# A hybrid convolution and RWKV-7 block on one core: the turns of even and odd chunks in the inverse's two merging bursts

## The chip, the cores and the metric

The kernel runs on one core of one Trainium2 chip. Its time is the device time of one execution in microseconds. The number given for a kernel is the median of several executions; the profile comes from one more execution. The engines are TensorE (PE, with its weight loads shown apart as PEld), VectorE (DVE), ScalarE (ACT), GpSimd (POOL) and SyncE (SP), which issues the transfers.

## The reference, cut to what matters

The block has 2048 tokens and 1024 channels. A normalised, modulated input goes through one wide projection. From it come a convolution branch (gate, causal depthwise convolution of width 31, layer norm) and an RWKV-7 branch with 16 heads of 64, whose state is updated token by token. Both are gated, projected, added, projected again, and normalised.

```python
def step(state, inp):
    r_t, w_t, k_t, v_t, kk_t, b_t = inp
    sk = jnp.einsum('bhvk,bhk->bhv', state, kk_t)
    state = (state * w_t[:, :, None, :] - sk[..., None] * b_t[:, :, None, :]
             + v_t[..., None] * k_t[:, :, None, :])
    return state, jnp.einsum('bhvk,bhk->bhv', state, r_t)
...
p = jnp.einsum('bsd,de->bse', h, w_in[l])
c_val, c_gate, c_og, ts, r_og, g_conv, g_rwkv = jnp.split(p, SPLITS, axis=-1)
y_conv = _conv_branch(c_val, c_gate, c_og, ...)
y_rwkv = _rwkv7_branch(ts, r_og, ...)
m = jax.nn.sigmoid(g_conv) * y_conv + jax.nn.sigmoid(g_rwkv) * y_rwkv
x = x + gate[:, None, :] * jnp.einsum('bsd,de->bse', m, w_out[l])
```

## The kernel before, in words

The tokens are worked on in four blocks of 512 (`TB`), the blocks in chunks of 64 tokens (`CH`, eight to a block), and the heads in four groups of four (`group`, two pairs `q` of two heads `hh`). So `group` runs sixteen times. Beside it, each block's wide projection and convolution are computed (`project`, `conv`, `gates`); the projection's products, `mm3k` at L205, are most of PE's instructions, and each weight tile of 128 columns is split into a high and a low part (`load_w`, L188 and L190). After the four blocks a second phase does the output projections.

Inside a chunk the recurrence is replaced by a triangular system: `As` holds, for each chunk, a 64 by 64 triangular matrix that has to be inverted. `group` does so for its 32 matrices (two pairs, two heads, eight chunks) at once:

- The two diagonal 32 by 32 blocks of each matrix go out to memory (`dA`, L610) and come back as `La`, where GpSimd inverts all of them together in 31 steps (L624, L626). The inverses go out again (`dT`) and come back into `As` (L637).
- The off-diagonal block of the inverse is the product of three 32 by 32 blocks. VectorE transposes one of the diagonal inverses into `T11` (L652, eight transposes, each for one pair, one head and the chunks of one parity). A first burst of 32 products on PE (L656) writes `pq`, a PSUM tile that the trace names `late`. VectorE copies it to `Qs` (L660, one copy per parity). A second burst of 32 products (L665) writes `pq` again, and VectorE copies the result into `As` (L670).
- Then the chunks are gone through one after another: L683, L685, L688, L690, L694 and L698 carry the state `S` on.

Even and odd chunks (`e`, 0 and 1) lie on different partitions. For an even chunk `quarters(e)` gives 64 to 95 and 96 to 127, for an odd one 0 to 31 and 32 to 63. The first burst reads from the first of the two ranges and writes to the second, the second burst the other way round.

The order of instructions on each engine is not the order of the text. A scheduler runs over the whole program, simulates the engines, and writes out the order that comes of it; on the chip each engine then executes its own list in order. So L205's products of the projection stand between the steps of the inverse and of the recurrence.

Of the kernel before, what the change touches and what calls it, by code (L numbers as in the profile page):

```python
# [82 lines left out]
def hybrid_block(ctx: ExitStack, tc: tile.TileContext, x, vecs, convk, w2a2, final_g, ada, w_in, w_co, w_ro, w_o, crow, out,  # L83
# [491 lines left out]
    def group(b, g, h, lora, fill):  # L575
# [14 lines left out]
        for c4 in range(NCH // 4):  # L590
            pv = pa.tile([P, 2, 2, P], F32, name="aux", tag="aux")
            for c in range(4 * c4, 4 * c4 + 4):
                e = c % 2
# [48 lines left out]
        def quarters(e):  # L642
            p0 = 64 - 64 * e
            return slice(p0, p0 + 32), slice(p0 + 32, p0 + 64)

        every = [(q, hh, c) for q in range(2) for hh in range(2) for c in range(NCH // 2)]
        pq = pl.tile([P, 2, 2, NCH // 2, 32], F32, name="late", tag="late")
        for e in range(2):
            lo_, hi_ = quarters(e)
            for q in range(2):  # L650
                for hh in range(2):
                    nc.vector.transpose(T11[lo_, q, hh], As[q][lo_, hh, e::2, lo_])  # L652
        for e in range(2):
            lo_, hi_ = quarters(e)
            for n, (q, hh, c) in enumerate(every):
                nc.tensor.matmul(pq[hi_, q, hh, c, :], As[q][lo_, hh, 2 * c + e, hi_], T11[lo_, q, hh, c, :],  # L656
                                 start=(n == 0), stop=(n == 15), skip_group_check=True)
        for e in range(2):
            lo_, hi_ = quarters(e)
            nc.vector.tensor_copy(Qs[hi_], pq[hi_])  # L660

        for e in range(2):
            lo_, hi_ = quarters(e)
            for n, (q, hh, c) in enumerate(every):
                nc.tensor.matmul(pq[lo_, q, hh, c, :], Qs[hi_, q, hh, c, :], As[q][hi_, hh, 2 * c + e, hi_],  # L665
                                 start=(n == 0), stop=(n == 15), skip_group_check=True)
        for e in range(2):
            lo_, hi_ = quarters(e)
# [5 lines left out]
        for c in range(NCH):  # L674
            cc, e = c // 2, c % 2
# [25 lines left out]
        for c4 in range(NCH // 4):  # L701
            po = pl.tile([P, 2, 2, P], F32, name="late", tag="late")
            with tc.issue_after(last.ins if hasattr(last, "ins") else last):
                for c in range(4 * c4, 4 * c4 + 4):
                    e = c % 2
# [166 lines left out]
    for b in range(NB):  # L872
        h = hprep(b) if b else hprep0(x0, ada_steps())
        lora = lora_split(h)
        for g in groups:
# [29 lines left out]

            wcount[0] = WSH
            group(b, g, h, lora, fill)
            if b == 0 and g == GG:
                for _ in ada_cols(srow, l3, "As", ASB, [((16 + k, 17 + k), (hgate_col[:, k:k + 1], hgate_col[:, k + 1:k + 2]))
# [138 lines left out]
    for b in range(NB):  # L1048
# [7 lines left out]
        for tt in range(NTT):  # L1056
            xh = []
            for half in range(2):
                n = 2 * tt + half
# [97 lines left out]
```

## Time and profile before

| what | us |
|---|---|
| median of three runs | 3070.52 |
| lowest and highest of them | 3058.14, 3070.98 |
| the profiled execution's own time | 3056.37 |
| its span, from first to last instruction | 3054.7 |
| PE busy | 2911.1 (95% of the span) |
| DVE busy | 2045.2 (67%) |
| POOL busy | 1257.3 (41%) |
| ACT busy | 1010.8 (33%) |
| PE busy with L656, 1024 records | 35.9 |
| PE busy with L665, 1024 records | 35.0 |

In the views of the profile a row of instructions gives the line in the kernel, the engine, the operation, what is written and read, the shape, and the count; "128*64" ahead of a shape is the part of the array in use, partitions by columns. An arrow names what ended the idle time ahead of an instruction. A product of float32 operands such as L656's stands there as two records, each with its own weight load.

### The profile page before, as it was taken

Reading aid. Unit: us, or ns where it says so; the run is one execution under the profiler, and the core shown is the slowest. Engines: PE = TensorE matmul, PEld = TensorE weight load, DVE = VectorE, ACT = ScalarE, POOL = GpSimd, SP = SyncE. Lnnn points to the kernel's source line nnn. Section 1 sums busy time; section 2 is a strip of 40 time slices with the busy share of each in tenths; the row PEclk is TensorE's granted clock in tenths of the full one; section 3 lists DMA queues with packets and bytes.
Section 4 is the critical chain, followed back from the end, with each engine's and each line's share of the span. In section 5 each row is a group of like instructions: output and inputs, shape, how many; then the busy total and the mean of one; then the engine's idle time right before and its main releaser. Section 6 shows DMA issues by size and latency. Waiting matters only on the chain.

```text
span 3054.7 us, 64810 instructions
## 1 busy us (share of the span) xinstructions
PE 2911.1 (95%) x25672; PEld 2754.0 (90%) x25672; DVE 2045.2 (67%) x3879; ACT 1010.8 (33%) x1887; POOL 1257.3 (41%) x1788
## 2 busy tenths in 40 slices
PE   6789998999999999999999999999999999899998
PEld 5789898999999998999999998999999978687988
DVE  6676877686766675767677667667689534767333
ACT  4424344433333242324242424232332112333101
POOL 3445455533443435243434355426276004555000
PEclk9999999999999999999999999999999999999999
DMA  8666757774747477648585888646457687989674
GB/s 300 220 233 199 250 198 260 242 236 152 243 142 257 140 248 239 194 139 273 161 276 168 274 276 271 199 157 204 154 184 243 199 277 281 325 294 339 235 277 171
DMA packets 366367, 697.14 MB, mean 228 GB/s; under 512 B 135984, under 2 KB 154736, under 8 KB 366064
## 3 DMA queue, kind: packets, MB, share of 16 engines
q1 hardware_dynamic: 366064, 693.00, 67.9%
q8 instruction: 202, 3.31, 0.5%
q14 instruction: 101, 0.83, 0.1%
HBM read 504.04 MB, written 187.70 MB: 226 GB/s over the span
## 4 chain that ended last, share of the span: by engine, by line
PE 57%; DMA 15%; DVE 12%; POOL 7%; ACT 3%; issue 3%; SPq 2%; DVEq 0%; ACTq 0%; POOLq 0%
PE ps_main L205 40%; DMA w_st<-w_in_t 3%; PE aux L537 3%; DVE acc L774 2%; POOL TT L626 2%; POOL itmp L624 2%; DMA w_gr<-grow_d 2%; DMA w_st<-w_co_t 2%; PE xo L688 2%; PE pout L1078 2%; PE pout L1079 2%; PE pout L1077 2%; DMA w_st<-w_ro_t 1%; PE xo L683 1%; PE xo L694 1%
## 5 line engine op out<-in xcount | busy, mean ns | idle before, releaser
L205 PE MATMUL ps_main<-h_hi,w_hi 128*128 128x256 f32 x4608 | 953.4, 285 | 24.3 <-ACT w_hi L188 16.1
L205 PE MATMUL ps_main<-h_hi,w_lo 128*128 128x256 f32 x4608 | 955.6, 285 | 9.6 <-POOL w_lo L190 6.5
L205 PE MATMUL ps_main<-h_lo,w_hi 128*128 128x256 f32 x4608 | 953.4, 284 | 0.0
L205 PEld LDWEIGHTS ps_main<-h_hi,w_hi 128*128 128x128 f32 x4608 | 718.8, 190 | 33.7 <-ACT w_hi L188 17.3
L205 PEld LDWEIGHTS ps_main<-h_hi,w_lo 128*128 128x128 f32 x4608 | 718.2, 190 | 18.3 <-POOL w_lo L190 7.7
L205 PEld LDWEIGHTS ps_main<-h_lo,w_hi 128*128 128x128 f32 x4608 | 717.7, 190 | 4.8 <-issue 0.2
L774 DVE SCALAR_TENSOR_TENSOR acc<-u,ck,acc 128x512 f32<-128x512 f32 x928 | 698.0, 752 | 19.4
L624 POOL TENSOR_TENSOR itmp<-La,TT 128x126 f32<-128x126 f32 (+22 forms) x496 | 181.9, 367 | 126.7 <-DMA La<-dA 91.1
L626 POOL TENSOR_TENSOR TT<-TT,itmp 128x126 f32<-128x126 f32 (+22 forms) x496 | 190.1, 383 | 36.6
L190 POOL TENSOR_TENSOR w_lo<-w_st,w_hi 128x1024 fp32r<-128x1024 f32 x47 | 113.1, 2407 | 116.5 <-ACT w_hi L188 94.6
L680 ACT ACTIVATE Se<-S,pe 128x128 f32<-128x128 f32 x256 | 89.0, 395 | 198.0 <-DVE S L698 196.9
L537 PE MATMUL aux<-KR,BKz 128*128 128x128 f32 x1024 | 137.9, 283 | 12.4 <-POOL KR L523 6.2
L698 DVE TENSOR_TENSOR S<-xo,Se 64x128 f32<-64x128 f32 x256 | 73.5, 287 | 107.6 <-PE xo L694 96.9
L537 PEld LDWEIGHTS aux<-KR,BKz 128*128 128x128 f32 x1024 | 126.9, 197 | 14.9 <-POOL KR L523 6.8
L188 ACT CAST w_hi<-w_st 128x1024 fp32r<-128x1024 f32 x71 | 74.3, 1047 | 195.9 <-DMA w_st<-w_in_t 159.3
L690 DVE TENSOR_TENSOR uv<-xo,rn 64x256 f32<-64x256 f32 x128 | 53.8, 421 | 103.0 <-PE xo L688 101.6
L539 DVE TENSOR_TENSOR As<-aux,maskA 128x512 f32<-128x512 f32 x128 | 87.3, 687 | 38.4 <-PE aux L537 37.3
L685 DVE TENSOR_TENSOR XO<-xo,XO 128x256 f32<-128x256 f32 x128 | 53.7, 419 | 86.1 <-PE xo L683 70.1
L560 POOL TENSOR_TENSOR vv<-rk,vv 128x512 f32<-128x512 f32 x32 | 43.9, 1372 | 154.3 <-ACT rk L559 148.0
L754 ACT ACTIVATE th<-ps_main 128x512 f32<-128x512 f32 x64 | 38.1, 596 | 206.8 <-PE ps_main L205 150.1
L531 ACT COPY BKz<-BK 64x512 f32<-64x512 f32 x128 | 78.9, 616 | 62.7 <-PE aux L537 39.7
L786 ACT ACTIVATE th<-ps_main 128x512 f32<-128x512 f32 x64 | 38.1, 595 | 182.8 <-PE ps_main L205 172.7
(301 smaller groups left out, 5530.9 us busy)
## 6 DMA issues: line engine op xcount, KB each, us to landing
w_hi<-kh_in SPq DMA_DIRECT2D x219, 512.0 KB, 4.2
w_lo<-kl_in SPq DMA_DIRECT2D x219, 512.0 KB, 5.4
w_st<-w_in_t SPq DMA_DIRECT2D x73, 512.0 KB, 4.7
kh_in<-w_hi SPq DMA_DIRECT2D x71, 512.0 KB, 2.9
kl_in<-w_lo SPq DMA_DIRECT2D x71, 512.0 KB, 4.8
w_hi<-kh_ro SPq DMA_DIRECT2D x32, 512.0 KB, 5.1
w_lo<-kl_ro SPq DMA_DIRECT2D x32, 512.0 KB, 6.1
w_hi<-kh_co SPq DMA_DIRECT2D x32, 512.0 KB, 3.9
```

The source lines that it names most:

```text
L188: nc.scalar.copy(hi, st)
L190: lo_eng.tensor_tensor(out=lo, in0=st, in1=hi.bitcast(F32), op=ALU.subtract)
L205: nc.tensor.matmul(ps[:, qs], ww[:, k, :], aa[k][:, qs], start=(k == 0 and t == 0 and q == 0), stop=(k == KT - 1 and t == 2 and q == ms - ...
L531: nc.scalar.copy(BKz[hs, hh], BK[hs, c4 * 2:c4 * 2 + 2])
L537: nc.tensor.matmul(pA[:, c // 2, es], BKz[:, hh, c // 2, es], KR[:, cc, es], start=(c == 0), stop=(c == 3), skip_group_check=True)
L539: nc.vector.tensor_tensor(out=Asb[:, hh, c4 * 4:c4 * 4 + 4, :].rearrange("p (a e) n -> p a (e n)", e=2), in0=pA, in1=flat(maskA).unsqueeze ...
L624: nc.gpsimd.tensor_tensor(out=tmp[:, :ni, :nt], in0=La[:, j:j + 1, j + 1:].broadcast_to([P, ni, nt]), in1=TT[:, :ni, j:j + 1].broadcast_to ...
L626: nc.gpsimd.tensor_tensor(out=TT[:, :ni, j + 1:], in0=TT[:, :ni, j + 1:], in1=tmp[:, :ni, :nt], op=ALU.add)
L680: nc.scalar.mul(Se[:, q, :], Sg[:, q, :], R[q]["pe"][:, c:c + 1])
L688: nc.tensor.matmul(xo[pr_, q, hs], As[q][pr_, hh, c, kcol(e)], XO[pr_, c, q, hs], start=(q == 0 and hh == 0), stop=(q == 1 and hh == 1), s ...
L698: nc.vector.tensor_tensor(out=Sg[hs, :, hs], in0=xo[hs, 2:4, hs], in1=Se[hs, :, hs], op=ALU.add)
L774: nc.vector.scalar_tensor_tensor(out=acc if i + 1 < HALO else yj, in0=u[:, i:i + TB], scalar=ck[:, j, i:i + 1], in1=acc, op0=ALU.mult, op1 ...
```

## The change

In each of the two bursts the loop over parities goes inside the loop over pair, head and chunk. The products are the same, with the same operands, the same places in `pq`, and the same first and last product for each parity. The transposes and copies around them are as they were.

```diff
-        for e in range(2):
-            lo_, hi_ = quarters(e)
-            for n, (q, hh, c) in enumerate(every):
+        for n, (q, hh, c) in enumerate(every):
+            for e in range(2):
+                lo_, hi_ = quarters(e)
                 nc.tensor.matmul(pq[hi_, q, hh, c, :], As[q][lo_, hh, 2 * c + e, hi_], T11[lo_, q, hh, c, :],
                                  start=(n == 0), stop=(n == 15), skip_group_check=True)
         for e in range(2):
             lo_, hi_ = quarters(e)
             nc.vector.tensor_copy(Qs[hi_], pq[hi_])
 
-        for e in range(2):
-            lo_, hi_ = quarters(e)
-            for n, (q, hh, c) in enumerate(every):
+        for n, (q, hh, c) in enumerate(every):
+            for e in range(2):
+                lo_, hi_ = quarters(e)
                 nc.tensor.matmul(pq[lo_, q, hh, c, :], Qs[hi_, q, hh, c, :], As[q][hi_, hh, 2 * c + e, hi_],
                                  start=(n == 0), stop=(n == 15), skip_group_check=True)
```

What the scheduler makes of it on PE, at the second burst of the third group of the first token block. A row is a product or a run of like ones; in brackets stand the engines or transfer queues that it waits for, here the transfers that brought that pair's and head's part of `As`. Before:

```order
L205 MATMUL ps_main<-h_hi,w_hi 128x256 x2
L665 MATMUL late<-As,Qs 32x32 [waits DMAHW2_49,DVE_49]
L665 MATMUL late<-As,Qs 32x32 x3
L665 MATMUL late<-As,Qs 32x32 [waits DMAHW3_49]
L665 MATMUL late<-As,Qs 32x32 x3
L665 MATMUL late<-As,Qs 32x32 [waits DMAHW3_49]
L665 MATMUL late<-As,Qs 32x32 x3
L665 MATMUL late<-As,Qs 32x32 [waits DMAHW4_49]
L665 MATMUL late<-As,Qs 32x32 x3
L665 MATMUL late<-As,Qs 32x32 [waits DMAHW7_49]
L665 MATMUL late<-As,Qs 32x32 x3
```

With the change:

```order
L205 MATMUL ps_main<-h_lo,w_hi 128x256 x2
L665 MATMUL late<-As,Qs 32x32 [waits DMAHW7_49,DVE_49]
L665 MATMUL late<-As,Qs 32x32 [waits DMAHW4_49]
L665 MATMUL late<-As,Qs 32x32 x6
L665 MATMUL late<-As,Qs 32x32 [waits DMAHW0_49]
L665 MATMUL late<-As,Qs 32x32 [waits DMAHW5_49]
L665 MATMUL late<-As,Qs 32x32 x6
L665 MATMUL late<-As,Qs 32x32 [waits DMAHW0_49]
L665 MATMUL late<-As,Qs 32x32 [waits DMAHW5_49]
L665 MATMUL late<-As,Qs 32x32 x6
```

Before, the first sixteen products are the even chunks', four for each pair and head, with one wait each. Now an even and an odd product stand one behind the other at each pair and head, so two waits follow each other, and then six products without any.

The first burst of the very first group stands in pieces among L205's products, on PE. Before:

```order
L205 MATMUL ps_main<-h_lo,w_hi 128x256 x2
L656 MATMUL late<-T_1570,As 32x32 [waits DVE_49]
L656 MATMUL late<-T_1570,As 32x32 x3
L656 MATMUL late<-T_1570,As 32x32 [waits DVE_49]
L656 MATMUL late<-T_1570,As 32x32 x3
L205 MATMUL ps_main<-h_hi,w_lo 128x256 [waits Pool_49]
```

With the change:

```order
L205 MATMUL ps_main<-h_lo,w_hi 128x256 x2
L656 MATMUL late<-T_1570,As 32x32 [waits DVE_49] x2
L656 MATMUL late<-T_1570,As 32x32 x7
L656 MATMUL late<-T_1570,As 32x32 [waits DVE_49]
L656 MATMUL late<-T_1570,As 32x32 x6
L205 MATMUL ps_main<-h_hi,w_lo 128x256 [waits Pool_49]
```

At the same place there stood eight even products, which wait for two transposes; now eight even and eight odd ones stand there, sixteen in all, and they wait for four. The first burst is in pieces in this group and in the second and third groups of the last token block, before and after; in the other thirteen groups, and in all second bursts, the 32 products stand together. Behind the first burst the scheduler's lists differ in many places on all engines, by rows that stand a little earlier or later; no row is lost or gained.

## The prediction

> **What bounds the kernel now.** I read the page's first part, then the table by stretches, then the timeline and the chain of waits around one pair of bursts.
>
> ```profile
> span 3054.7 us, 64810 instructions
> PE 2911.1 (95%) x25672; PEld 2754.0 (90%) x25672; DVE 2045.2 (67%) x3879; ACT 1010.8 (33%) x1887; POOL 1257.3 (41%) x1788
> 200.00:650.00 450.00, 424.77 (x4041) 410.83 (x4041) 335.39 (x581) 177.51 (x298) 235.28 (x307) 0.96 0.69 230
> 650.00:2450.00 1800.00, 1763.80 (x17207) 1711.71 (x17206) 1271.05 (x2401) 607.54 (x1143) 768.01 (x1240) 0.99 0.65 210
> ```
>
> In the last two rows the first number after the length is PE's busy time. PE is idle for 25.2 of 450 us and then for 36.2 of 1800 us. All sixteen groups lie in these 2250 us, and PE's own queue sets the pace there: an instruction taken off PE is time, unless a wait that is there anyway takes it back.
>
> The two bursts of a group, here the third of the first token block, look so on PE's timeline (start, length with the last instruction's own end, count), on the vector engine's, and in the chain (start, time that the piece adds):
>
> ```profile
> 529.58 0.40 PE L205 MATMUL ps_main<-h_hi,w_lo 128*128 128x256 f32 x2
> 529.81 0.39 PE L205 MATMUL ps_main<-h_hi,w_hi 128*128 128x256 f32 x2
> 530.14 2.11 PE L656 MATMUL late<-T,As 32*32 32x32 f32 x64
> 532.17 0.63 PE L505 MATMUL aux<-bones,sq 128*64 128x2 f32 x16
> 532.74 0.51 PE L205 MATMUL ps_main<-h_lo,w_hi 128*128 128x256 f32 x2
> 537.76 2.11 PE L665 MATMUL late<-As,Qs 32*32 32x32 f32 x64
> ...
> 532.28 1.40 DVE L660 COPY Qs<-late 32x512 f32<-32x512 f32 x2 [3.06 <-PE late L656]
> ...
> 530.21 2.04 PE late L656 x64
> 537.83 2.04 PE late L665 x64
> ```
>
> A product of 32 by 32 stands in the trace as two records, so 32 products are 64. Both bursts lie whole on the chain. The even and the odd half's copies start at 532.28, after the last odd product (530.14 + 2.11 = 532.25): the even half's being ready at half time is not used today.
>
> **What the burst would take with turns.** An even product uses partitions 64 to 95 and writes 96 to 127, an odd one 0 to 31 and 32 to 63 (the second burst the other way round): two separate pieces of the array. Three narrow looks at the same burst show what separate pieces do; each row holds what runs within a 10 ns window, at the middle of the even products, at the change from even to odd, and at the middle of the odd ones:
>
> ```profile
> L656 PE MATMUL late<-T,As x1024: 191/191/212, 195.7 to 2418.1; 32*32 32x32 f32 x171
> L665 PE MATMUL late<-As,Qs x1024: 191/191/257, 205.2 to 2424.0; 32*32 32x32 f32 x171
> 530.41 0.38 PE L656 MATMUL late<-T,As 32*32 32x32 f32 x7
> 530.98 0.38 PE L656 MATMUL late<-T,As 32*32 32x32 f32 x10
> 531.42 0.38 PE L656 MATMUL late<-T,As 32*32 32x32 f32 x7
> ```
>
> One record takes 0.19 us, so in the first row seven start within 0.38 - 0.19 us: six gaps of 31.7 ns. At the change ten start in the same time: the last even and the first odd records run together. A second place in this kernel alternates all the way, the sums of L505, whose chunks go in turn to the two halves of the output; L688 has weights of the same 64 columns and stays on one piece:
>
> ```profile
> 2002.23 0.68 PE L688 MATMUL xo<-XO,As 64*64 64x64 f32 x8
> L688 PE MATMUL xo<-XO,As x1024: 218/218/366, 207.9 to 2516.4; 64*64 64x64 f32 x171
> L505 PE MATMUL aux<-bones,sq x512: 197/198/268, 73.4 to 2286.0; 128*64 128x2 f32 x171
> ```
>
> L688: (0.68 - 0.22) / 7 = 66 ns a record. L505: (0.63 - 0.20) / 15 = 29 ns. Alternating there halves the time, over a whole burst and not only at an edge.
>
> **The sum, part by part.** Nothing is removed or added: the 1024 products, the transposes, the copies and every transfer stay.
>
> First, the bursts. With both pieces at their own rate, each does 32 records: 31 x 31.7 ns + 0.19 us = 1.17 us, with a slower first step 1.2. That is 0.91 us less than 2.11, and there are 32 bursts: -29.1 us. The low end of the gain is PE handing out records no faster than in L505: 63 x 28.7 ns + 0.19 = 2.0 us, 0.11 less, -3.5 us in all. I take the upper end, since the row at the change has 9 gaps in 0.19 us, 21 ns on average, although some of these gaps lie outside the overlap.
>
> The Trainium skill ("TensorE: Matmul & The Clock Gate", section "Wait — 56ns, not 53.3ns?") says that start to start never drops under about 25 ns, however small the product. By it a burst would be 63 x 25 ns + 0.19 = 1.8 us (an estimate from that page) and the change worth -11 us; the 21 ns above speak against it, over ten records only.
>
> Second, the waits. An interleaved first burst needs the odd transposes (L652) as early as the even ones. Where the burst stands late this costs nothing: the third group's last transpose (the last row below) ends 34 us before its burst. In three groups the order starts the burst while transposes are still coming: the first of all, and two in the last token block. Rows of the first (vector engine, then PE), of the last block's third, and for comparison of the third group of the first block:
>
> ```profile
> 195.31 0.49 DVE L652 STREAM_TRANSPOSE T<-As 32x128 f32<-32x128 f32 x2 [2.84 <-DMA As<-dT]
> 196.05 0.63 DVE L652 STREAM_TRANSPOSE T<-As 32x128 f32<-32x128 f32 x2 [0.25 <-DMA As<-dT]
> 195.67 0.69 PE L656 MATMUL late<-T,As 32*32 32x32 f32 x16
> ...
> 2270.02 1.35 DVE L652 STREAM_TRANSPOSE T<-As 32x128 f32<-32x128 f32 x5
> 2275.85 0.29 DVE L652 STREAM_TRANSPOSE T<-As 32x128 f32<-32x128 f32 x1
> 2270.52 0.69 PE L656 MATMUL late<-T,As 32*32 32x32 f32 x16
> ...
> 495.99 0.29 DVE L652 STREAM_TRANSPOSE T<-As 32x128 f32<-32x128 f32 x1
> ```
>
> In the first group the eight products that start at 195.67 need the two transposes of 195.31; with turns that place holds sixteen, which need four, the last done at 196.68. PE stands for up to 0.9 us, with the L205 products of that weight tile queued behind it. For the three groups I take 3 us. Low end 0 (the rest of the fill covers it). High end: PE standing from the burst's start to the last transpose, 2276.14 - 2270.52 = 5.6 us, in each of three, 17 us. I stay near the low end because the rows behind the first products are L205's in every one of them.
>
> Third, the copies. Qs's and As's copies start after the last product already, so nothing is lost by the even half's finishing late; they and all that follows (L665, then L688 of the recurrence) start 0.9 us earlier per burst. If the copies of the even half had been early, 0.7 us of cover (half of 1.40) would be gone in each burst; between the bursts PE has L205 work, 5 us in the third group.
>
> Fourth, what is given back. Saved PE time is lost where PE meets a wait that its own progress doesn't feed. Low end 0. High end: the idle time of 61 us grows by a quarter, 15 us. With 3 groups in the stretch that is 5.6% idle and 13 in the one that is 2.0% idle, I take 3 us, the idle share of the gain (0.056 x 5.5 + 0.02 x 23.7 = 0.8) with room for the rest.
>
> Not in the sum, but in the range: the granted clock.
>
> ```profile
> 530.10:533.80 3.70, 3.70 (x90) 3.61 (x90) 1.48 (x3) 1.76 (x2) 1.84 (x1) 1.00 1.01 314
> 533.80:537.20 3.40, 3.40 (x17) 3.21 (x16) 2.29 (x6) 2.24 (x4) 3.23 (x4) 0.50 0.95 252
> core 0: 3054.7 us, clock 0.982
> ```
>
> Right after this first burst PE has 0.50 of its clock for 3.4 us, a loss of 1.7 us. Shorter bursts may make such stretches rarer or only shift them; four more or fewer are 7 us.
>
> Sum against the profiled execution's own 3056.4 us (span 3054.7 and 1.7 around it): 3056.4 - 29.1 + 3 + 3 = 3033. The runs shown lie on two levels, 3058 and 3071, with the median on the upper one: by it the sum is 3070.5 - 23 = 3047. I name the middle, 3040 us.
>
> **The rivals.**
>
> A. Handing out is the limit, at L505's 29 ns. For: L505 is the longest alternating stretch there is, and it goes no faster. Against: its weights are twice as wide, so 29 ns is also just half of its own piece's rate. -3.5 to -6 us: 3051 on the profile's level, 3065 on the median's. Not to be told from no change.
>
> B. The order takes the gain back. The scheduler sets a new order on every engine behind the first burst. For: PE's 61 us of idle time come from waits that a shifted row can lengthen. Against: no row is lost or gained, the fills between the steps of the recurrence have about as many L205 products as before, and the recurrence's waits are short today. PE's waits for its state, and for the transposes (total, times, longest):
>
> ```profile
> PE xo L683 <- DVE S L698: 9.0, 7, 3.0
> PE late L656 <- DVE T L652: 1.0, 4, 0.3
> ```
>
> If waits grow by a third, 20 us, the time is 3056 - 26 + 20 = 3050 (3064); only if they grow by half is it slower.
>
> C. Each change between pieces costs something, and nothing overlaps. From L205 to the first record takes 530.14 - 529.81 = 0.33 us for two records where 0.23 is usual (529.81 - 529.58), 0.10 more for a change of shape. At that price 31 changes a burst are 3.1 us, in 32 bursts +99 us: 3155. It decides from 15 ns a change on (15 x 31 x 32 = 15 us). Against: L505 changes at every product and is the faster for it.
>
> D. Both halves write the same tile `late`, and the writes exclude each other. Then every record waits its turn at 31.7 ns, and the overlap at the change is gone as well: 64 x 31.7 + 0.19 = 2.2 us, +0.1 a burst, +3 us: 3060 (3074). Against: in the row of ten both halves write this tile. The Trainium skill has such a rule ("TensorEngine Tiling (Array Packing)", section "Gotcha 1: PSUM Pressure": row tiles can't use one bank at the same time); by it this change could only lose, and the trace disagrees where the two pieces also differ in their output partitions.
>
> That the order undoes the turns is excluded: the built program has them in all 32 bursts, three of them in pieces.
>
> **How the numbers follow.** Forecast 0.67, A 0.10, B 0.14, C 0.05, D 0.04. A measurement can't tell less than 0.5%, 15 us. The forecast's own span, 23 +- 8, on either level runs from 3026 to 3055, all of it faster. A and D are within 0.5%; of B's 0.14 I put 0.02 on faster, 0.09 on the same, 0.03 on slower; C is slower. Faster 0.69, same 0.23, slower 0.08. The range goes from 3021 (the lower level with all of the gain and some clock) to 3063 (the upper level with A or B).
>
> **What would show it.** A burst should be a row of 64 records in 1.2 us instead of 2.11, at both lines, and a narrow look at any place of it should hold 12 or more records instead of 7. PE's busy time should be 25 to 30 us less, at an unchanged number of instructions. L652 as PE's releaser should grow from 1.0 us to a few. L660's copies should start right after a burst that is 0.9 us shorter. If the burst is 1.7 us or more, A or D holds; over 2.2, C; if it is 1.2 and the time has hardly moved, B, and PE's idle time in the 2250 us is then well over 61.

## The result: the bursts are as short as forecast, and the time is half a percent longer

The changed kernel takes 3080.09 us (median of seven runs, 3072.81 to 3084.47), the kernel before 3069.58 beside it. The ratio is 1.0048, 95% interval 1.0031 to 1.0064. Forecast were 3040 us in a range of 3021 to 3063: the sign is wrong and the range misses. The profiled execution of the change took 3082.34 us.

The page's first rows and the table by stretches, of the change (length, then busy time of PE, its weight loads, DVE, ACT and POOL, then the granted clock):

```profile
span 3080.3 us, 64815 instructions
PE 2905.4 (94%) x25672; PEld 2744.3 (89%) x25672; DVE 2065.1 (67%) x3879; ACT 1010.3 (33%) x1887; POOL 1254.0 (41%) x1788
200.00:650.00 450.00, 423.92 (x4047) 408.65 (x4047) 342.74 (x586) 177.08 (x298) 234.59 (x307) 0.96 0.67 228
650.00:2450.00 1800.00, 1745.57 (x17057) 1690.67 (x17056) 1269.02 (x2389) 602.23 (x1134) 765.00 (x1240) 0.98 0.64 207
core 0: 3080.3 us, clock 0.972
```

In the 2250 us of the sixteen groups PE is now idle for 26.1 + 54.4 = 80.5 us, where it was 61.4, and the mean clock of the whole span has gone from 0.982 to 0.972. PE's busy time is 5.7 us less, not 25 to 30: at half clock the same work counts as more busy time (below, L688's eight records take 1.02 us instead of 0.68).

The bursts, on PE's and DVE's timelines of the change, at the same group as in the prediction. The last two rows are narrow looks of 10 ns, one into a burst of each line:

```profile
532.45 1.20 PE L656 MATMUL late<-T,As 32*32 32x32 f32 x64
533.58 0.63 PE L505 MATMUL aux<-bones,sq 128*64 128x2 f32 x16
...
535.07 1.39 DVE L660 COPY Qs<-late 32x512 f32<-32x512 f32 x2
540.83 1.53 DVE L670 COPY As<-late 32x256 f32<-32x256 f32 x4
...
532.81 0.38 PE L656 MATMUL late<-T,As 32*32 32x32 f32 x13
2277.33 0.36 PE L665 MATMUL late<-As,Qs 32*32 32x32 f32 x12
```

A burst takes 1.20 us instead of 2.11, with 12 or 13 records in a look where there were 7. So it is in 26 of the 32; two more fall into a stretch of half clock (1.92 us), and four first bursts are in pieces or wait for transposes on the way. PE's busy time with the two lines falls from 70.9 to 42.8 us, by 28.1. So the first term of the sum holds, and the question is where these 28 us, and 10 more, have gone.

**Where it shows most.** The third group of the last token block, on PE and then DVE, with the change:

```profile
2276.96 1.20 PE L665 MATMUL late<-As,Qs 32*32 32x32 f32 x64
2282.06 1.02 PE L688 MATMUL xo<-XO,As 64*64 64x64 f32 x8 [3.90 <-DVE As L670]
2283.01 2.07 PE L537 MATMUL aux<-KR,BKz 128*128 128x128 f32 x8
2285.27 2.08 PE L537 MATMUL aux<-KR,BKz 128*128 128x128 f32 x8 [0.18 <-ACT ta L474]
2287.14 1.06 PE L694 MATMUL xo<-uv,tk 128*128 128x128 f32 x4
2290.85 3.90 PE L537 MATMUL aux<-KR,BKz 128*128 128x128 f32 x16 [2.66 <-DVE As L539]
2294.41 0.77 PE L205 MATMUL ps_main<-h_hi,w_hi 128*128 128x256 f32 x2
...
2281.58 1.53 DVE L670 COPY As<-late 32x256 f32<-32x256 f32 x4
```

Behind the second burst PE has no product of L205 for 2294.41 - 2278.16 = 16.2 us. It stands 3.90 us until DVE, which is 3.4 us late with its copy (2281.58), gives As free, then it works at half speed: eight records of L688 take 1.02 us, where the prediction has 0.68. DVE's lateness isn't new: in the kernel before this copy starts 3.5 us behind the burst (2283.28 + 2.11 and then the row below), but there PE has L205 products in the meantime.

```profile
2283.28 2.11 PE L665 MATMUL late<-As,Qs 32*32 32x32 f32 x64
2288.87 1.53 DVE L670 COPY As<-late 32x256 f32<-32x256 f32 x4
```

Two stretches of 10 us at the place with the change, and then the 18 us behind the burst's end, with the change and before:

```profile
2275.00:2285.00 10.00, 6.10 (x94) 5.29 (x92) 9.86 (x16) 4.31 (x7) 2.85 (x2) 0.84 0.30 107
2285.00:2295.00 10.00, 7.16 (x32) 6.74 (x32) 9.83 (x17) 3.70 (x8) 3.52 (x3) 0.50 0.00 0
...
2278.16:2296.16 18.00, 11.26 (x53) 10.51 (x54) 17.77 (x28) 6.61 (x12) 6.28 (x5) 0.62 0.12 49
```

```profile
2285.40:2303.40 18.00, 16.92 (x141) 16.45 (x142) 17.76 (x33) 8.29 (x14) 11.87 (x9) 0.91 0.62 204
```

DVE is busy for 17.8 of 18 us in both. PE is busy for 16.9 us before and for 11.3 with the change, at a clock of 0.91 and of 0.62. Here DVE sets the pace, and what PE gets done beside it depends on what its list offers. The lists of PE at this place, before and then with the change:

```
L665 MATMUL late<-As,Qs 32x32 x32
L505 MATMUL aux<-bones,sq 64x2 x8
L205 MATMUL ps_main<-h_hi,w_hi 128x256 x2
(sixteen more rows of L205)
L688 MATMUL xo<-XO,As 64x64 x2
```

```
L665 MATMUL late<-As,Qs 32x32 x32
L688 MATMUL xo<-XO,As 64x64 x4
L537 MATMUL aux<-KR,BKz 128x128 x8
L694 MATMUL xo<-uv,tk 128x128 x2
L537 MATMUL aux<-KR,BKz 128x128 x8
L205 MATMUL ps_main<-h_hi,w_hi 128x256 x2
```

The theory after the result: the turns are worth the 29 us that were forecast for the bursts; the scheduler's new lists take it back, above all at this place. The rivals: the turns themselves cost something elsewhere, or any new list does.

### The profile page after: what moved, and what is told of

It reads as the page before. It is cut to its first block, busy times and chain, and to the rows that moved or that the text cites. A ratio compares the mean times of both kernels' runs of the same rounds, so it can differ in the third digit from the quotient of the medians.

```text
span 3080.3 us, 64815 instructions
## 1 busy us (share of the span) xinstructions
PE 2905.4 (94%) x25672; PEld 2744.3 (89%) x25672; DVE 2065.1 (67%) x3879; ACT 1010.3 (33%) x1887; POOL 1254.0 (41%) x1788
## 4 chain that ended last, share of the span: by engine, by line
PE 57%; DMA 13%; DVE 12%; POOL 8%; issue 4%; SPq 3%; ACT 3%; POOLq 0%; DVEq 0%; ACTq 0%
PE ps_main L205 40%; PE aux L537 3%; POOL itmp L624 3%; POOL TT L626 3%; DMA w_st<-w_in_t 2%; PE xo L688 2%; PE pout L1077 2%; PE pout L1079 2%; PE pout L1078 2%; DVE acc L774 2%; DMA w_gr<-grow_d 1%; PE xo L683 1%; DMA La<-dA 1%; SPq L637 1%; PE xo L694 1%
## 5 line engine op out<-in xcount | busy, mean ns | idle before, releaser
L205 PE MATMUL ps_main<-h_hi,w_hi 128*128 128x256 f32 x4608 | 961.0, 286 | 36.4 <-ACT w_hi L188 22.7
L205 PE MATMUL ps_main<-h_hi,w_lo 128*128 128x256 f32 x4608 | 959.0, 286 | 12.8 <-DMA w_lo<-kl_in 8.1
L205 PE MATMUL ps_main<-h_lo,w_hi 128*128 128x256 f32 x4608 | 961.2, 286 | 0.0
L205 PEld LDWEIGHTS ps_main<-h_hi,w_hi 128*128 128x128 f32 x4608 | 724.7, 191 | 47.0 <-ACT w_hi L188 24.3
L205 PEld LDWEIGHTS ps_main<-h_hi,w_lo 128*128 128x128 f32 x4608 | 722.1, 191 | 22.4 <-DMA w_lo<-kl_in 10.2
L205 PEld LDWEIGHTS ps_main<-h_lo,w_hi 128*128 128x128 f32 x4608 | 723.8, 191 | 5.9 <-issue 0.2
L537 PE MATMUL aux<-KR,BKz 128*128 128x128 f32 x1024 | 140.4, 287 | 10.7 <-ACT BKz L531 6.8
L949 POOL TENSOR_TENSOR ot<-ot,bt 128x512 f32<-128x512 f32 x24 | 34.7, 1447 | 155.1 <-DMA bt<-bv_d 150.1
```

The costliest lines, as they stand in the source:

```text
L205: nc.tensor.matmul(ps[:, qs], ww[:, k, :], aa[k][:, qs], start=(k == 0 and t == 0 and q == 0), stop=(k == KT - 1 and t == 2 and q == ms - ...
L537: nc.tensor.matmul(pA[:, c // 2, es], BKz[:, hh, c // 2, es], KR[:, cc, es], start=(c == 0), stop=(c == 3), skip_group_check=True)
```

## The experiments

The runs separate the two things that the change does, the turns and the lists. Lists are held by a function that puts an issue-order edge, without a wait, from each instruction of an engine to the next one in a given list:

```diff
         hybrid_block(tc, *args, out)
+        pinned(tc)
...
+def pinned(tc):
+    have = {i.name: i for i in tc.nc.cur_bb.bb.instructions}
+    for part in zlib.decompress(base64.b85decode(ORDER)).decode().split("|"):
+        last, at = None, 0
+        for d in part.split(":")[1].split(","):
+            at += int(d)
+            i = have.get(f"I-{at}")
...
+            if last is not None:
+                tc.add_manual_dep(i, last.name, mybir.DependencyInfo(mybir.DependencyClass.NoSync, mybir.DependencyReason.DATA),
+                                  reason="pinned")
+            last = i
```

`ORDER` is a packed table of instruction numbers; the diffs below say in words what it holds.

### The turns in the old lists, and the new lists without turns

The first kernel is the change with the lists of before; the second is the kernel before with the change's lists.

```diff
+ORDER = (lists of before; code of the change)
```

> The change's bursts, with every engine's list held in the order it had before, down to the instruction; inside a burst alone even and odd products take turns. Theory 'order' (the shorter bursts are worth their time, and what was lost after the change comes from the scheduler's new lists): 3070 - 32 x 0.91 = 3041, and not over 3050. Rival 'nothing behind it needs the time' (PE's saved time turns into waits or into a lower clock, whatever the order): 3060 to 3085, with PE's idle time between 200 and 2450 us up by 20 us or more and the bursts at 1.20 us all the same.

Measured: 3055.46 us, ratio 0.9945 [0.9927, 0.9964]. That lies between the two readings, over the 3050 of the theory and under the 3060 of the rival. The lists do take the gain away, but without them the turns are worth 17 us and not 29, so a part of the saved time turns into waits in the old lists as well.

```diff
+ORDER = (lists of the change; code of before)
```

> The other way round: every engine's list in the order that it has with the change, but inside each burst all even products ahead of the odd ones, as before. Theory 'order': slower than the change by what the bursts take, 3080 + 25 to 29 = 3105 to 3109. Rival 'nothing behind it needs the time': within 8 us of the change, 3072 to 3088.

Measured: 3106.77 us, ratio 1.012 [1.0099, 1.0141]. The change's lists alone cost 1.2%, about 37 us; in them the turns are worth 1.012 - 1.0048 = 0.7%, 22 us, and in the old lists 0.55%, 17 us. So the turns are a gain in either list, and the lists more than take it.

### Holding the lists, and another new list

The kernel before with its own lists held, and the kernel before with only the parities exchanged in both bursts (odd half first), from which the scheduler makes lists of its own:

```diff
+ORDER = (lists of before; code of before)
```

> The kernel before with its own lists held by the same edges: the same program, instruction for instruction. Every theory: 3068, ratio 1.000 within 0.002. It gives a second profile of the kernel before and shows that holding the lists costs nothing.

Measured: 3062.0 us, ratio 0.9995 [0.9979, 1.001]. The held lists cost nothing that can be told (0.2%), so the two runs above measure turns and lists and not the holding.

```diff
-        for e in range(2):
+        for e in (1, 0):
             lo_, hi_ = quarters(e)
             for n, (q, hh, c) in enumerate(every):
                 nc.tensor.matmul(pq[hi_, q, hh, c, :], As[q][lo_, hh, 2 * c + e, hi_], T11[lo_, q, hh, c, :],
...
-        for e in range(2):
+        for e in (1, 0):
             lo_, hi_ = quarters(e)
             for n, (q, hh, c) in enumerate(every):
                 nc.tensor.matmul(pq[lo_, q, hh, c, :], Qs[hi_, q, hh, c, :], As[q][hi_, hh, 2 * c + e, hi_],
```

> The kernel before with the odd chunks' products ahead of the even ones in both bursts, no turns; the scheduler makes its own lists, which again differ from those before in thousands of rows. A burst takes 2.11 us as before. Theory 'order' (the lists alone move the time by tens of us): not bound to be near 3070; 3055 to 3100. Rival (lists that differ by such small shifts do not matter, turns cost something): 3070, within 5 us.

Measured: 3067.95 us, ratio 0.9999 [0.9981, 1.0017]. A new list need not cost anything. It is what stands in the change's lists that does.

### Turns in the second burst only

```diff
-        for e in range(2):
-            lo_, hi_ = quarters(e)
-            for n, (q, hh, c) in enumerate(every):
+        for n, (q, hh, c) in enumerate(every):
+            for e in range(2):
+                lo_, hi_ = quarters(e)
                 nc.tensor.matmul(pq[lo_, q, hh, c, :], Qs[hi_, q, hh, c, :], As[q][hi_, hh, 2 * c + e, hi_],
```

> Turns in the second burst alone, lists made anew by the scheduler. A second burst takes 1.20 us, a first one 2.11. Theory 'order': anything from 3050 to 3095, not bound to lie between the kernel before and the change. Rival 'turns cost what they save': half of the change's loss, 3074, within 4.

Measured: 3079.59 us, ratio 1.0052 [1.0032, 1.0072], with lists of the scheduler's own again. That is more than the rival by which turns cost what they save allows (3074, within 4). The earlier transposes that the first burst needs aren't what makes the change slow: the kernel with the turns in the old lists needs them too and is faster than before, and here, without turns in the first burst, the time is as long as with the change. Behind the second burst of the last block's third group 48 L205 records start within 18 us; before there were 88 and with the change 9 (counted from the traces).

### Which part of the lists

Two kernels with the turns change from one set of lists to the other at the 12131st L205 product, on every engine at a place where all that the earlier part needs has been issued. On the chip that product starts at 2118 to 2129 us in the kernels made so (called 2120 below); the 2170 us in the expectations are a miscount of mine.

```diff
-ORDER = (lists of before)
+ORDER = (lists of the change up to the 12131st L205 product, then lists of before)
```

> Turns in both bursts; the lists of the change up to about 2170 us (the second group of the last token block), then the lists of before. In the profiles the change and the run with turns on the old lists are level there, and the change loses 22 us in the 90 us that follow, where its PE list has no projection product between the second burst of the last block's third group and the recurrence's third step. Theory 'the loss sits in that group': 3055, like the run with turns on the old lists, within 8. Rival 'the loss is spread over all groups of the new lists': 3080 less a quarter of the 25, 3074.

Measured: 3059.45 us, ratio 0.9989 [0.9971, 1.0008].

```diff
-ORDER = (lists of before)
+ORDER = (lists of before up to the 12131st L205 product, then lists of the change)
```

> The other half: turns in both bursts, the lists of before up to the same place, then those of the change. Theory 'the loss sits in that group': 3080, within 8. Rival 'spread': 3055 plus a quarter of 25, 3061.

Measured: 3073.93 us, ratio 1.0025 [1.001, 1.0041]. Between the change (1.0048) and the turns in the old lists (0.9945) lie 0.0103, about 32 us. By these two runs the change's lists behind 2120 us are worth 0.0059 (1.0048 - 0.9989) or 0.0080 (1.0025 - 0.9945) of it, and those of the first 2120 us 0.0023 to 0.0044, 7 to 13 us. Each of these differences is uncertain by some 0.0025, so a third of the program's length holds more than half of the cost, some two thirds at best guess.

### The one place

The old lists throughout, except for the stretch with that third group (2120 to 2300 us), on one chip with a second measurement of the turns in the old lists:

```diff
-ORDER = (lists of before)
+ORDER = (lists of before, of the change from the 12131st to about the 13020th L205 product, then of before)
```

> The change's turns in the lists of before, except for one stretch: from about 2170 to 2340 us every engine follows the change's lists, then those of before again. Theory (one place: behind the second burst of the last block's third group PE has no L205 product to do for 16 us): PE loses the 22 us there that it lost with the change, so the ratio to before lies 0.007 over that of turns in the old lists alone (0.9945), at 1.001 to 1.003; behind that burst the L205 products of the next 18 us are about 7 records and not 88. Rival (the new lists cost a little everywhere): a stretch of 170 of 3080 us costs a twentieth of 38 us, 2 us, ratio 0.995 to 0.996, with or without those products.

> The change's turns in the lists of before throughout, a second time and on the same chip as the two kernels with one stretch exchanged, as their measure: ratio 0.993 to 0.996 if the first measurement (0.9945) holds, both theories alike.

Measured: 3065.91 us, ratio 0.9995 [0.9983, 1.0008], for the one, and 3051.16 us, ratio 0.9945 [0.9927, 0.9963], for the other. A stretch of 180 us costs 0.0050, uncertain by some 0.002, or 15 us; the theory had said 22, the rival 2. Measured by when the nth L205 product starts, the two profiles are 1.4 us apart at the 12100th and 14.9 at the 13150th, and 14 to 18 to the end. PE in that stretch of the kernel with the place, and two stretches of 10 us of it:

```profile
2269.15 1.20 PE L665 MATMUL late<-As,Qs 32*32 32x32 f32 x64
2274.33 1.11 PE L688 MATMUL xo<-XO,As 64*64 64x64 f32 x8 [3.98 <-DVE As L670]
2275.37 4.24 PE L537 MATMUL aux<-KR,BKz 128*128 128x128 f32 x16
...
2286.05 0.77 PE L205 MATMUL ps_main<-h_hi,w_hi 128*128 128x256 f32 x2
...
2265.00:2275.00 10.00, 6.02 (x101) 5.48 (x96) 9.83 (x17) 3.91 (x6) 4.55 (x6) 0.84 0.38 137
2275.00:2285.00 10.00, 7.14 (x36) 6.30 (x35) 9.86 (x19) 3.67 (x7) 3.58 (x3) 0.67 0.00 0
```

The wait for DVE, the 15.7 us without L205 and the lower clock are all there. Without the place, in the turns with the old lists, PE has its fill behind the burst:

```profile
2282.33 1.20 PE L665 MATMUL late<-As,Qs 32*32 32x32 f32 x64
2284.03 0.63 PE L505 MATMUL aux<-bones,sq 128*64 128x2 f32 x16 [0.51 <-ACT sq L501]
2285.37 0.50 PE L205 MATMUL ps_main<-h_hi,w_hi 128*128 128x256 f32 x2 [0.71 <-DVE carry L438]
...
2285.00:2295.00 10.00, 9.63 (x67) 9.23 (x68) 9.87 (x20) 3.58 (x6) 7.04 (x5) 0.83 0.56 175
```

So this place is enough, in the old lists, for half of what the lists cost.

### The mirror, which failed

The change's lists with only this stretch from before's:

```diff
-ORDER = (lists of the change)
+ORDER = (lists of the change, of before from the 12131st to about the 13020th L205 product, then of the change)
```

> The mirror of the kernel before it: the change's turns in the change's lists, except that from about 2170 to 2340 us every engine follows the lists of before. Theory (one place): the 22 us are not lost, ratio 0.007 under that of the change (1.0048), at 0.997 to 0.999, and 85 or more L205 records in the 18 us behind that burst. Rival (a little everywhere): 1.004.

Measured: 3082.13 us, ratio 1.0048 [1.0029, 1.0067]; no gain. PE's timeline shows that the second switch fell into the place:

```profile
2286.63 1.20 PE L665 MATMUL late<-As,Qs 32*32 32x32 f32 x64
...
2290.19 0.28 PE L205 MATMUL ps_main<-h_hi,w_lo 128*128 128x256 f32 x1
2290.40 0.67 PE L688 MATMUL xo<-XO,As 64*64 64x64 f32 x8
2291.59 0.71 PE L694 MATMUL xo<-uv,tk 128*128 128x128 f32 x4 [0.52 <-DVE uv L690]
2293.80 0.71 PE L683 MATMUL xo<-S,KR 128*128 128x128 f32 x4 [1.49 <-DVE S L698]
2295.83 1.11 PE L688 MATMUL xo<-XO,As 64*64 64x64 f32 x8 [1.32 <-DVE XO L685]
2298.39 1.22 PE L694 MATMUL xo<-uv,tk 128*128 128x128 f32 x4 [1.45 <-DVE uv L690]
2300.46 1.20 PE L683 MATMUL xo<-S,KR 128*128 128x128 f32 x4 [0.84 <-DVE S L698]
2301.31 0.56 PE L205 MATMUL ps_main<-h_hi,w_lo 128*128 128x256 f32 x1
```

From 2290 us on two steps of the recurrence run with no L205 product between them, because the products that the change's list has there were already issued. It is another gap of the same kind, and the run tells nothing on the question. A second try put both switches at places where the two lists have done nearly the same work:

```diff
-ORDER = (lists of the change)
+ORDER = (lists of the change, of before from the 11900th to the 14000th L205 product, then of the change)
```

> The mirror once more, with both changes of list at places where the two lists have done nearly the same work: the change's turns in the change's lists, except that from the 11900th to the 14000th L205 product (about 2090 to 2450 us) every engine follows the lists of before. In the mirror run before, the second change of list fell 4 us behind the burst in question, and the L205 products that stand between the next steps of the recurrence were lost there as well (11 us without one). Theory (the loss sits where L205 products are missing, most of it in this stretch): the gaps of over 2 us between L205 products from 2170 to 2340 us add up to 23 to 28 us again, as in before, and not 37 to 42, and the ratio falls from 1.0048 to 0.998 to 1.0005. Rival (a little everywhere): 360 of 3080 us, 12% of 38 us, 4 to 5 us, ratio 1.003 to 1.0035.

Measured: 3076.65 us, ratio 1.0046 [1.0026, 1.0065]. In the profile the place is healed: from the 12200th to the 13900th L205 product PE takes 289.5 us, where it takes 306.2 with the change and 288.7 and 287.8 in the two profiles of the turns in the old lists. The total isn't better all the same. Behind the second switch two more steps stand without fill:

```profile
2450.83 0.61 PE L694 MATMUL xo<-uv,tk 128*128 128x128 f32 x4
2452.29 0.68 PE L683 MATMUL xo<-S,KR 128*128 128x128 f32 x4 [0.85 <-DVE S L698]
2453.49 0.68 PE L688 MATMUL xo<-XO,As 64*64 64x64 f32 x8 [0.52 <-DVE XO L685]
2454.68 0.72 PE L694 MATMUL xo<-uv,tk 128*128 128x128 f32 x4 [0.52 <-DVE uv L690]
2456.25 1.19 PE L683 MATMUL xo<-S,KR 128*128 128x128 f32 x4 [0.85 <-DVE S L698]
2457.09 0.77 PE L205 MATMUL ps_main<-h_lo,w_hi 128*128 128x256 f32 x2
```

The last run has that switch and the end alone:

```diff
-ORDER = (lists of before)
+ORDER = (lists of before up to the 14000th L205 product, then lists of the change)
```

> The change's turns in the lists of before until the 14000th L205 product (about 2450 us), and in the change's lists from there: the end of the kernel e11, alone. It tells why e11 was no faster than the change although its exchanged stretch lost 2 us and not 23. Right behind this second change of list two steps of the recurrence stand without an L205 product between them (the change's list has them earlier, that of before later). If the switch and the last 600 us are what e11 lost again: ratio 0.9995 to 1.001 (0.9945 and the 0.0057 by which e11 stands over e4, which differs from it only from there on), and 9 us lost in the profile in the 150 L205 products behind the 13900th. If the lists of the first 2090 us were it (one profile of e11 was 11 us longer there): ratio 0.9955 to 0.9965, by the 4 us that the change itself loses behind 2450 us.

Measured: 3058.64 us, ratio 0.9979 [0.9965, 0.9993]: 0.0034, 10 us, over the turns in the old lists, halfway between what the two readings said. The second reading in its expectation rests on an artefact: at the 12100th product the change's list is ahead for a moment, and 100 products later that is gone. Counted at the 12200th and the 13900th product, the profiles of the kernel with the exchanged stretch and of the change differ by +3.3 us in the first part, -16.7 in the middle and +9.0 in the last (13.5 us behind the turns in the old lists instead of 4.5): -4.4 in all, as their spans say (3075.9 and 3080.3). A difference of 4 us, 0.0014, can't be seen in the timed runs. So the place was healed there, and a good half of it was lost again by the second switch. That the change would be faster with this place alone healed is thus seen in one stretch of a profile and not in a timed total. What the timed runs show is that the place alone makes the old lists slower by 15 us, and that taking everything behind 2120 us from before's lists wins 18 us (0.0059). Of the 32 us that the change's lists cost beside the old ones, then, about half is this place, by the run with the place in the old lists; the rest is spread (7 to 13 us of it in the first 2120 us) and was not followed to single places.

## Why the prediction was wrong, by its own steps

A balance first. It counts PE's idle time from the 1000th to the last L205 product (length less PE's busy time) and the time lost at half clock over the whole span (half the length of the stretches that the clock record gives at 0.50). The kernel before stands as the mean of its two profiles, one with the lists held:

| kernel | span | PE idle | lost at half clock |
|---|---|---|---|
| before, two profiles | 3054.7, 3066.2 | 79.1, 82.4 | 54.8, 64.4 |
| turns, old lists, two profiles | 3056.9, 3048.8 | 100.2, 92.9 | 60.7, 66.3 |
| turns, new lists (the change) | 3080.3 | 104.4 | 87.9 |
| halves, new lists | 3105.4 | 104.2 | 81.8 |

For the change: -29.1 (bursts) + 23.6 (idle) + 28.2 (clock) = +22.7, and the span is 19.9 longer than the mean before. For the halves in the new lists: 23.4 + 22.2 = 45.6, and 45.0 are measured. For the turns in the old lists it is -9.4 on the mean of two profiles, of which the spans show -7.5; the timed runs say -17, and single profiles scatter by that much (the two of the kernel before differ by 11.5). The balance is rough. Half-clock time in which PE stands idle counts in both columns (in the stretch of the idle column, half-clock time with PE busy grows by 21.7 us with the change, not 28.2), and over the other eight profiles the same sum misses the span by 3 to 11 us.

With the old lists the number would have held: 0.9945 of 3069.58 is 3053 us, inside the range, and the gain of 17 us lies within the 23 +- 8 of the forecast. In part that is luck, for the idle time grew by 16 us there, and the sum has 3 + 3. The starting level is a smaller error: the seven runs of the kernel before lie all the way between 3058 and 3071 and show no two levels, and from their median the sum would have been 3047 and not 3040.

**What bounds the kernel**: right for most of the 2250 us, wrong where it mattered. In the third group of the last block DVE is busy for 17.8 of 18 us, and there, by the rows of the place, a shorter burst on PE wins nothing. The table by stretches of 1800 us had averaged this away.

**First, the bursts, -29.1**: right, 1.20 us at full clock, and 28.1 us less of PE's busy time. Rivals A, C and D fall with it: 64 records in 1.20 us are (1.20 - 0.19) / 63 = 16.0 ns a record, below L505's 29, with no cost of a change between pieces, while both pieces write the same tile.

**Second, the waits for early transposes, +3**: right. PE's waits for L652 with the change (first row), and three others that grew:

```profile
PE late L656 <- DVE T L652: 4.9, 6, 1.7
PE xo L688 <- DVE As L670: 5.5, 2, 3.9
PE ps_main L205 <- ACT w_hi L188: 22.7, 5, 9.1
PE ps_main L205 <- DMA w_hi<-kh_in: 8.3, 5, 2.9
```

The first row grew from 1.0 to 4.9. The second was 0.6 before, and the longer of its two times is the place above. The last two are L205's waits for its weights, 16.1 and nothing before.

**Third, the copies**: the step "start 0.9 us earlier per burst" is wrong for the second burst in the old lists. It is DVE that is late next. DVE's wait for L665's products, before and then with the turns in the old lists:

```profile
DVE As L670 <- PE late L665: 7.9, 9, 2.1
```

```profile
DVE As L670 <- PE late L665: 2.3, 4, 1.1
```

Before, DVE waited for the second burst in nine of sixteen groups, 7.9 us in all (11.0 in the other profile). No more than that could be won on its side. Measured from a burst's end to its first copy, summed over the sixteen groups, DVE was 6.6 and 7.0 us late before, and is 20.6 and 18.4 with the turns in the old lists, 13 us more, while the sixteen bursts are 15.1 us shorter. So the copies of the second burst come 2 us earlier in all, not 15. The first burst's copies do better, their lateness goes from 7 to 10 us. With the change's own lists the second burst's copies are 10.7 us late in all, 4 more than before, so there most of the 15.8 us saved reaches DVE.

PE's idle time in the old lists is 16 us more on the mean, close to the upper end of 15 that the prediction's fourth term had and did not take. The late copies are not shown to be its cause: PE's own waits for L670 grew by 2.2 us there, and the rest is spread over many rows, 3.3 us of it the waits for transposes.

**Fourth, what is given back, +3, and rival B at 0.14**: this is the step that failed. The prediction's own sign for B came: a burst of 1.20 us, a time that has hardly moved, and 80.5 us of idle time in the 2250 us where there were 61.4. The +3 was sized from the idle share of long stretches, and B was made harmless by the sentence that "the fills between the steps of the recurrence have about as many L205 products as before". That held for most fills and not for one. Between a second burst and the first L688 behind it stand 8 to 34 L205 products before, in all groups but the very first, which has none. With the change it is 17 to 27, but the last block's third group has none either, where there were 34, and in the 18 us behind that burst 88 L205 records had become 9. The lists cost 1.0 to 1.2%, more than the turns win. B's mechanism was the right one, but its price was read from the recurrence's waits for its state (9.0, with the change 11.2), while half of the growth of PE's waits in the trace (132.6 to 162.9 us) is in L205's waits for its own inputs (48.8 to 65.0). And "only if they grow by half is it slower" was wrong too: the idle time of the 2250 us grew by a third, and the time was slower, because the clock came on top.

**The clock, four stretches or 7 us**: mis-sized. The half-clock loss grew by 28 us, or 22 with PE busy, about as much as the idle time. The two go together in the rows of the place (6.10 of 10 us busy, then a clock of 0.50), and the stretch with the place in the old lists has them as well. The Trainium skill ("TensorE: Matmul & The Clock Gate", "What's actually happening") says that the clock is gated to half after an idle window of about 3.4 us; the 3.90 us wait for As agrees, with the clock at 0.50 from 2282.30 us on, 0.2 us behind its end. An idle window doesn't explain the prediction's own rows, where 0.50 followed on 3.70 us in which PE was busy throughout.

Idle time and slower work have no fixed ratio here. With the turns in the old lists 16 us more of idle time came with 4 us of half-clock loss, with the change 24 came with 28. Between these two, the same turns in two sets of lists, the difference is mostly the clock: 8 us of idle time and 24 of half-clock loss. The timed runs show it too: the median granted clock is 0.972 over the seven runs of the change, and 0.980 over the fourteen of the turns in the old lists.

## What to carry to other kernels

When an edit makes a scheduler write new lists, cost the lists as a part of the change, and look at the shortest fill behind each long wait and not at the typical one: one gap of 16 us in a stretch where another engine sets the pace took back half of what 32 shorter bursts had saved. Count what a lost fill does to the clock beside the idle time. Ask how long the next engine waited for the work that becomes faster: DVE waited 7.9 us for the second bursts before, and of 15 us saved there some 2 reached its copies in the old lists. Keep the two apart by measurement: the same turns with the old lists held beat both kernels (3051 to 3055 us, ratio 0.9945 twice).

## What the runs showed of the hardware

Two pieces of the array with different rows and different output columns run float32 products of 32 by 32 side by side at their full rate: 64 records in 1.20 us, 16.0 ns each where one piece alone took 31.7, sustained over the whole burst and with both writing one PSUM tile. The Trainium skill ("TensorE: Matmul & The Clock Gate", "Wait — 56ns, not 53.3ns?") states a floor of about 25 ns from start to start; it doesn't hold here. The rule of the Trainium skill that row tiles can't use one bank at the same time ("TensorEngine Tiling (Array Packing)", "Gotcha 1: PSUM Pressure") wasn't seen where the pieces also differ in their output partitions.

A single profile is worth about 10 us here: the kernel before and the same kernel with its lists held have spans of 3054.7 and 3066.2 us, at a timed ratio of 0.9995, and the first 11950 L205 products, with the same turns and the same lists in five of the kernels, took times up to 10 us apart. Where that comes from was not tried.
